# Two token streams on one core: another order for convolution, attention and MLP of the second stream

## The chip, the cores and the metric

The kernel runs on one core of one Trainium2 chip. A core has five engines that work beside each other and meet at semaphores: TensorE (PE: matmuls), VectorE (DVE), ScalarE (ACT), GpSimd (POOL) and SyncE (SP, which here issues DMA transfers). Each engine takes its own instructions strictly in the order in which the program put them into its queue. The metric is the device time of one execution in microseconds. Three timed runs of the kernel before gave a median of 3942.52 us (3938.76 to 3944.16).

## What is computed

One inference step of a two-layer decoder for a prompt of 1024 tokens and eight samples of eight tokens. Cut to its core:

```
for layer in (0, 1):
    x += conformer_conv(rms_norm(x))  if layer == 0 else  rwkv7_time_mix(rms_norm(x))
    x += cross_attend(rms_norm(x), memory K/V of the layer)     # 4 heads, 256 memory tokens
    x += sq_relu_mlp(rms_norm(x))                               # 1024 -> 4096 -> 1024
y = rms_norm(x)
```

The convolution module is a product 1024 -> 2048 with a gate, a causal depthwise convolution of 31 taps, a LayerNorm, and a product 1024 -> 1024. The RWKV module is a set of products (r, k, v and low-rank ones), a recurrence over positions with a 64x64 state per head (the scan), and an output product. All values are fp32; weights that are read for several products are split into a high and a low part, and each product is three matmuls (high by high, high by low, low by high).

## The kernel before, in words

The 1088 tokens are cut in two parts. Part 1 (512 tokens) is stream A, part 2 (576 tokens: 512 of the prompt and the 64 of the samples) is stream B. Activations lie with channels on the partitions; a matmul takes a 128x128 piece of a weight and 256 (A) or 288 (B) tokens. A product over 1024 channels is 24 such matmuls into one PSUM bank (`prod`, lines 126 to 128), then an evacuation on ACT or DVE. A weight tile of 128x1024 comes by a 512 KB DMA, ACT rounds it (line 95) and DVE or POOL takes the remainder (line 96).

Each stream runs through the same stages, one after the other. Names as used below, with the lines that show in the profile:

- convolution (`convolve`: fp32 matmuls L345 and L425 on PE, the other taps as 25 or 23 DVE passes per channel group, L441 and L444), then its output (`conv_out`: a LayerNorm, L470 to L490, and a product whose bank is added to x by DVE, L496);
- first attention (`attention`: for each of 8 units scores, softmax, four transposes L541, output; then a product added to x by DVE L288; stream B has the samples' caches besides, L590 to L593, and needs 32 more weight tiles for them);
- first MLP (`mlp`: 3,072 matmuls per stream; up banks through ACT L692, POOL L694 and the pair `u`, down banks added to x by DVE L708);
- the inputs of the RWKV module (`projections`: norm, token mixing on POOL, DVE and ACT, three products of 384 matmuls each, and low-rank products L792 and L841);
- the scan (lines 1070 to 1500: banks `p_pp`, `p_pz`, `p_py`; units of 2 head pairs and 256 tokens, 8 for A, 8 and one for the samples for B; the second matmul of a unit's last step, L1441, is used below as the mark of its end);
- memory keys of layer 1 (A alone), output product, second attention, second MLP and the last norm.

The streams are two generators. `pace` calls the one whose clock is behind; what a generator yields is the cost that is added to its clock, and `scaled` multiplies it:

```
i = min(ready, key=lambda i: clock[i])
c = next(gens[i], "end")
clock[i] += c
```

Stream B's factors stand in `CONV_COST` (convolution and its output) and `B_COST` (first attention, first MLP, RWKV inputs, output, second attention). A larger factor means that B is called less often beside the same piece of A. B's scan waits for the end of A's scan. The order of these calls is the order of priority; a scheduler then places the instructions of each engine, and may put a later one first where an earlier one isn't ready by its own reckoning. The scan is emitted 1000 places ahead in priority. So the tables set an order, not a time, and what stands in the queues has to be read from the built program.

Of the kernel before, what the change touches and what calls it, by code (L numbers as in the profile page):

```python
# [155 lines left out]
def body(tc, nc, es, a, o):  # L156
# [37 lines left out]
    def use_part(ctx, s, name):  # L194

        n = PARTS[s.part][1]
        s.use_ring([(s.pool(ctx, "ring" + name), "w", RING.get(s.name + name, 2))])
        hp = s.pool(ctx, "part" + name)
        s.x1 = hp.tile([P, NC8, 1 + n], F32, name="x" + s.name + name)
        s.x = xt[s.part] = s.x1[:, :, 1:]  # L200
        s.hp = hp
# [5 lines left out]
    def load_x(part, src, tiles=None):  # L207
        for t0, n in tiles or PARTS[part][2]:
            nc.sync.dma_start(out=xt[part][:, :, t0:t0 + n], in_=src[:, :, t0:t0 + n])
# [721 lines left out]
    def prior(gen, key):  # L931
        by = AHEAD.get(key, 0)
        return ahead(gen, by) if by else gen

    def scaled(gen, by):
        for c in gen:
            yield c if isinstance(c, str) else by * (1.0 if c is None else c)
# [12 lines left out]
    def conv_layer(s):  # L950
        with ExitStack() as ph:
            s.phase(ph, "c", d=4)
            cq = s.pool(ph, "cq")
            yield from convolve(s, cq, s.part)
            yield f"conv{s.part}!"
            yield from conv_out(s, s.part, pair(s))

    def att_layer(s, l, **k):
        with ExitStack() as ph:
            s.phase(ph, f"a{l}", **(dict(d=2, sa=2) if s.part else dict(d=4)))  # L960
            ap = s.pool(ph, f"at{l}")
            yield from attention(s, ap, l, s.part, pair(s), 1, (ap, "kv", 1))

    def mlp_layer(s, l):
        with ExitStack() as ph:
            s.phase(ph, f"m{l}", d=4 if s.part or l == 0 else 4)
            u = s.pool(ph, f"u{l}").tile([P, 2, 4, PARTS[s.part][1]], F32R, name="u")
            if l and s.part:
                s.use_ring(s.ring + [(s.pool(ph, "rx"), "w", 2)])
            yield from mlp(s, l, s.part, pair(s), u)  # L970
            if l:
                yield from final(s, s.part)

    def rwkv_in(s):
        with ExitStack() as ph:
            yield from projections(s, ph, s.part, pair(s))
# [6 lines left out]
    def rwkv_out(s):  # L983
        with ExitStack() as ph:
            s.phase(ph, "wo", d=4)
            yield from mixer_out(s, s.pool(ph, "yl"), s.part, pair(s))
# [27 lines left out]
    def second():  # L1014
        s = sB
        with ExitStack() as ph:
# [8 lines left out]
            load_x(1, a["x"][:, :, 512:])  # L1025
            yield from scaled(prior(conv_layer(s), "convB"), CONV_COST)
            yield OFFSET
            yield from scaled(prior(att_layer(s, 0), "att0B"), B_COST[0])
            yield "att0B!"
            yield from scaled(prior(mlp_layer(s, 0), "mlp0B"), B_COST[1])  # L1030
            yield "mlp0B!"
            yield from scaled(prior(rwkv_in(s), "inB"), B_COST[2])
            yield "in0B!"
# [3 lines left out]
        with ExitStack() as ph:  # L1037
            use_part(ph, s, "1")
            yield from scaled(prior(rwkv_out(s), "outB"), B_COST[3])
            yield from scaled(prior(att_layer(s, 1), "att1B"), B_COST[4])  # L1040
            yield "att1B!"
# [6 lines left out]
TAP_COST = 0.353  # L1048
OFFSET = 5.0
SCAN_COST = [1.344, 1.248]  # L1050
B_COST = [1.1, 1.0, 1.075, 1.04, 0.85]
MLP_COST = 1.0
EVERY = {'Bc': 4, 'Aa0': 3}
RAWS = 4
# [6 lines left out]
MEM_COST = 3.0  # L1061
MEM1 = True
SCAN_AHEAD = 1000
CONV_COST = 0.96
TMP = dict(A=dict(acc=2, sq=2, rs=2, h=2, sg=2, ev=2, dl=2, st=2), B=dict(h=2, sg=2, ev=2, sq=2), Bp=dict(dl=2, st=2), Bm0=dict(sg=2))
PE_PAIRS = (4, 3)
BUF = dict(w=5, ld=1, Z2=2, bon=2, ar=2, Aq=2, UV=2, AV=2, BK=1, pcs=2)
# [604 lines left out]
```

## Time and profile before

| | |
|---|---|
| median of three runs | 3942.52 us |
| the profiled execution | 3943.05 us, its span 3941.3 us |
| PE busy | 3729.5 us (95%), 29898 matmuls |
| DVE, ACT, POOL busy | 62%, 41%, 21% |
| mean granted TensorE clock | 0.949 of full |

A time axis in the text is microseconds from the start of the span. Matmul records overlap, so a busy PE is not one at its peak: the number of matmuls in a stretch (x) and the granted clock (1.00 is 2.4 GHz, 0.50 is 1.2 GHz, in between a mix of both) say more than the busy share. Stages of stream A by the first and last of their matmuls: convolution and its output 14 to 372, first attention to 674, first MLP to 1303, RWKV inputs to 1743, scan to 2337. B's scan ends at 3026.

### The profile page before, as it was taken

The numbers are of one execution on the slowest core, as the hardware profiler recorded it, in microseconds if no ns is written. First come the engines' busy times: TensorE is split into PE (matmuls) and PEld (weight loads), VectorE is DVE, ScalarE is ACT, GpSimd is POOL, SyncE is SP. The second block draws the span as 40 slices with busy tenths as digits, with TensorE's granted clock in tenths as the row PEclk, the third lists the DMA queues.
The fourth block names the chain that finished last, engine by engine and source line by source line (L and its number), as shares of the span: only waits on it lengthen the run. The fifth ranks groups of instructions, "written<-read, shape, count | busy, mean of one in ns | idle before, by whom it ended". The sixth has DMA issues, their size and how long they took to land. (4 is left out here: it accounts for less than half of the span.)

```text
span 3941.3 us, 74158 instructions
## 1 busy us (share of the span) xinstructions
PE 3729.5 (95%) x29898; PEld 3440.5 (87%) x29898; DVE 2456.6 (62%) x4800; ACT 1628.7 (41%) x3347; POOL 844.6 (21%) x1084
## 2 busy tenths in 40 slices
PE   8989979999999999998999978898999999999998
PEld 7757769999999999998788756787889999999998
DVE  7889964556554765457787736867774445753334
ACT  3233253445333444444465543454544335532222
POOL 0010121024101333211464311222121003301110
PEclk9999989999999999999699968898999999999998
DMA  6424223245322333332133326322223335532221
GB/s 220 129 57 136 72 83 110 83 136 186 118 79 93 117 118 120 123 124 93 55 111 100 103 83 225 111 68 76 69 79 121 116 104 164 169 99 81 84 83 52
DMA packets 231864, 428.64 MB, mean 109 GB/s; under 512 B 42848, under 2 KB 151648, under 8 KB 231520
## 3 DMA queue, kind: packets, MB, share of 16 engines
q1 hardware_dynamic: 202592, 392.95, 31.2%
q10 hardware_dynamic: 27648, 26.75, 2.0%
q8 instruction: 235, 3.85, 0.4%
q0 software_dynamic: 1280, 4.20, 0.3%
q14 instruction: 109, 0.89, 0.1%
HBM read 354.43 MB, written 60.91 MB: 105 GB/s over the span
## 5 line engine op out<-in xcount | busy, mean ns | idle before, releaser
L96 DVE TENSOR_TENSOR wt<-raw,wt 128x1024 fp32r<-128x1024 f32 x471 | 599.2, 1275 | 414.0 <-ACT wt L95 411.9
L95 ACT CAST wt<-raw 128x1024 fp32r<-128x1024 f32 x512 | 533.6, 1047 | 493.1 <-PE B_d L128 249.0
L126 PE MATMUL B_d<-hAB,wt 128*128 128x288 f32 (+1 forms) x2240 | 674.6, 304 | 18.4 <-ACT hAB L95 7.1
L127 PE MATMUL B_d<-hBB,wt 128*128 128x288 f32 (+1 forms) x2240 | 673.0, 301 | 6.6 <-DVE hBB L96 6.4
L128 PE MATMUL B_d<-hAB,wt 128*128 128x288 f32 (+1 forms) x2240 | 668.4, 299 | 2.3 <-DVE wt L96 2.3
L126 PE MATMUL A_d<-hAA,wt 128*128 128x256 f32 x2240 | 640.6, 289 | 24.2 <-ACT hAA L95 21.4
L128 PE MATMUL A_d<-hAA,wt 128*128 128x256 f32 x2240 | 633.2, 285 | 14.1 <-DVE wt L96 11.9
L127 PE MATMUL A_d<-hBA,wt 128*128 128x256 f32 x2240 | 639.5, 287 | 6.4 <-DVE hBA L96 6.4
L126 PEld LDWEIGHTS A_d<-hAA,wt 128*128 128x128 f32 x2240 | 427.9, 192 | 40.1 <-ACT hAA L95 26.7
L126 PEld LDWEIGHTS B_d<-hAB,wt 128*128 128x128 f32 x2240 | 427.7, 192 | 29.3 <-ACT hAB L95 10.9
L128 PEld LDWEIGHTS A_d<-hAA,wt 128*128 128x128 f32 x2240 | 427.4, 192 | 20.9 <-DVE wt L96 13.0
L127 PEld LDWEIGHTS A_d<-hBA,wt 128*128 128x128 f32 x2240 | 428.3, 192 | 19.6 <-DVE hBA L96 9.0
L127 PEld LDWEIGHTS B_d<-hBB,wt 128*128 128x128 f32 x2240 | 429.8, 192 | 11.7 <-DVE hBB L96 9.1
L694 POOL TENSOR_TENSOR t_sg<-t_ev 128x256 f32<-128x256 f32 (+1 forms) x256 | 184.8, 722 | 1160.3 <-ACT t_ev L692 1096.5
L128 PEld LDWEIGHTS B_d<-hAB,wt 128*128 128x128 f32 x2240 | 429.3, 192 | 4.0 <-DVE wt L96 2.9
L126 PE MATMUL B_d<-u,wt 128*128 128x288 f32 x1024 | 302.1, 296 | 0.7 <-DVE xB L708 0.7
L127 PE MATMUL B_d<-u,wt 128*128 128x288 f32 x1024 | 301.5, 296 | 0.0
L128 PE MATMUL B_d<-u,wt 128*128 128x288 f32 x1024 | 300.9, 296 | 0.4 <-DVE wt L96 0.4
L128 PE MATMUL A_d<-u,wt 128*128 128x256 f32 x1024 | 287.8, 283 | 0.7 <-DVE wt L96 0.7
L127 PE MATMUL A_d<-u,wt 128*128 128x256 f32 x1024 | 288.1, 282 | 0.0
L126 PE MATMUL A_d<-u,wt 128*128 128x256 f32 x1024 | 287.3, 283 | 0.0
L96 DVE TENSOR_TENSOR u<-t_sg,u 128x256 fp32r<-128x256 f32 (+1 forms) x256 | 131.6, 516 | 140.7 <-ACT u L95 140.4
(401 smaller groups left out, 7545.8 us busy)
## 6 DMA issues: line engine op xcount, KB each, us to landing
raw<-in_mlp_up_dram SPq DMA_DIRECT2D x128, 512.0 KB, 3.4
raw<-in_mlp_dn_dram SPq DMA_DIRECT2D x128, 512.0 KB, 3.4
raw<-in_rw_w_dram SPq DMA_DIRECT2D x64, 512.0 KB, 3.5
ld<-scr SPq DMA_DIRECT2D x32, 640.0 KB, 5.5
wf<-in_w_in_dram SPq DMA_DIRECT2D x32, 512.0 KB, 3.5
raw<-in_xa_w_q_dram SPq DMA_DIRECT2D x32, 512.0 KB, 3.4
raw<-in_xa_w_o_dram SPq DMA_DIRECT2D x32, 512.0 KB, 3.5
raw<-in_ck_dram SPq DMA_DIRECT2D x32, 512.0 KB, 3.5
```

The lines of the kernel that those rows point to most:

```text
L95: self.nc.scalar.copy(hi, src)
L96: (engine or self.nc.vector).tensor_tensor(lo, src, hi.bitcast(F32), SUB)
L126: self.nc.tensor.matmul(out, lhsT=wh, rhs=mh, start=(i == 0), stop=False)
L127: self.nc.tensor.matmul(out, lhsT=wh, rhs=ml, start=False, stop=False)
L128: self.nc.tensor.matmul(out, lhsT=wl, rhs=mh, start=False, stop=(i == last))
L694: nc.gpsimd.tensor_mul(sg[:, :n], r[:, :n], r[:, :n])
```

## The change

Three numbers of the tables, and nothing else:

```
-B_COST = [1.1, 1.0, 1.075, 1.04, 0.85]
+B_COST = [0.9, 0.5, 1.075, 1.04, 0.85]
-CONV_COST = 0.96
+CONV_COST = 2.0
```

B's convolution and its output are called at about half the rate, its first attention at 1.22 times and its first MLP at twice the rate; the factors of the later stages stay. No instruction is added or removed: each engine has the same instructions in another order. Three places in the built programs follow. In all of them A_ and xA are stream A's banks and residual, B_ and xB stream B's.

The first place is DVE's queue where B's convolution output is added to x (L496). Before, it stands among A's attention (L525 to L534 are a softmax, `pr` and `hBA<-A_d` the unit's splits):

```order
L487 TENSOR_TENSOR xB_145<-xB_145,t_rs 128x288 x8
L525 TENSOR_REDUCE st_3896<-A_d 128x2
L496 SCALAR_TENSOR_TENSOR xB_145<-B_d,vec,xB_145 128x288
L96 TENSOR_TENSOR hBB<-t_h,hAB 128x288 x2
L529 RECIPROCAL st_3896<-st_3896 128x2
L534 TENSOR_SCALAR e<-e,st_3896 128x256 x2
L496 SCALAR_TENSOR_TENSOR xB_145<-B_d,vec,xB_145 128x288
```

In the changed program the first of them stands among the down products of A's first MLP (L708):

```order
L708 TENSOR_TENSOR xA_103<-xA_103,A_d 128x256 x4
L96 TENSOR_TENSOR wt<-raw,wt 128x1024
L496 SCALAR_TENSOR_TENSOR xB_145<-B_d,vec,xB_145 128x288
L96 TENSOR_TENSOR u<-t_sg,u 128x256
L96 TENSOR_TENSOR wt<-raw,wt 128x1024
L96 TENSOR_TENSOR u<-t_sg,u 128x256 x2
L496 SCALAR_TENSOR_TENSOR xB_145<-B_d,vec,xB_145 128x288
```

All 384 matmuls of B's convolution output moved behind the first matmul of A's first MLP; before, 264 of them stood in front of the last one of A's first attention. The convolution itself did not move: PE's queues agree but for a few neighbours up to place 1823, which the trace of before reaches at 544 us, and that is behind the last of B's convolution.

The second place is PE's queue at the end of the third unit of A's scan (`p_` rows are the scan's). Before, B's RWKV inputs stand between its rows (`hAB`, `hBB`, and the low-rank `B_hd`):

```order
L126 MATMUL B_d<-hAB,wt 128x288
L1441 MATMUL p_py<-rs,c_bones 128x512
L1329 MATMUL p_pp<-td,Ybd 128x16 x8
L792 MATMUL B_hd<-hc,w_21397 128x288
L792 MATMUL B_hd<-hc,w_21397 64x288
L127 MATMUL B_d<-hBB,wt 128x288
```

Now B's first MLP stands there (`u`):

```order
L126 MATMUL B_d<-u,wt 128x288
L1441 MATMUL p_py<-rs,c_bones 128x512
L127 MATMUL B_d<-u,wt 128x288
L128 MATMUL B_d<-u,wt 128x288
L126 MATMUL B_d<-u,wt 128x288
L127 MATMUL B_d<-u,wt 128x288
L1329 MATMUL p_pp<-td,Ybd 128x16 x8
```

Of the 3,084 matmuls of B's first MLP and its norm 551 stand behind the first matmul of A's scan before, and 1,837 now.

The third place is PE's queue at the end of A's scan. Before, memory keys of stream A follow at once:

```order
L1389 MATMUL p_py<-Aq,UV 64x64 x2
L1436 MATMUL p_py<-y,c_bones 128x512
L1441 MATMUL p_py<-rs,c_bones 128x512
L126 MATMUL A_d<-hAA,wt 128x256 x2
L127 MATMUL A_d<-hBA,wt 128x256
```

Now the rest of B's RWKV inputs follows:

```order
L841 MATMUL B_d<-lh,w_23724 128x288
L1441 MATMUL p_py<-rs,c_bones 128x512
L792 MATMUL B_hd<-hc,w_23585 64x288
L792 MATMUL B_hd<-hc,w_23694 128x288
L792 MATMUL B_hd<-hc,w_23694 64x288
L126 MATMUL B_d<-hAB,wt 128x288
```

397 of the 1,436 matmuls of B's RWKV inputs stand behind the end of A's scan now, none before.

Split matmuls (those that read a weight tile `wt`) in front of the end of each scan unit, counted from the one before it, in both programs; the first count starts at the first matmul of A's scan:

| end of unit | before | after |
|---|---|---|
| A 1 | 551 MLP B | 605 MLP B |
| A 2, 3, 4 | 60, 334, 230 inputs B | 329, 358, 321 MLP B |
| A 5 | 198 inputs B | 224 MLP B |
| A 6, 7, 8 | 186, 144, 0 inputs B | 401, 223, 240 inputs B |
| samples | 288 memory A, 83 output A | 288 inputs B, 288 memory A, 384 output A |
| B 1 | 301 output A, 114 attention A | 411 attention A |
| B 2, 3, 4, 5 | 282, 96, 135, 333 attention A | 81, 164, 304 attention A, 324 MLP A |
| B 6, 7, 8 | 285, 330, 382 MLP A | 371, 354, 343 MLP A |

## Rows read from the trace of the kernel before

**Rows 1.** Page, parts 1 and 2: busy time, PE and granted clock in 40 slices
```profile
PE 3729.5 (95%) x29898; PEld 3440.5 (87%) x29898; DVE 2456.6 (62%) x4800; ACT 1628.7 (41%) x3347; POOL 844.6 (21%) x1084
...
PE   8989979999999999998999978898999999999998
...
PEclk9999989999999999999699968898999999999998
```

**Rows 2.** Busy time by stage: stretch, length, each engine's us, clock, DMA
```profile
14.00:372.00 358.00, 334.61 (x1706) 265.56 (x1707) 311.82 (x528) 116.29 (x262) 24.79 (x45) 0.97 0.40 125
372.00:674.00 302.00, 270.45 (x1682) 231.89 (x1680) 219.02 (x391) 113.96 (x235) 56.48 (x46) 0.93 0.29 93
674.00:1303.00 629.00, 623.38 (x5060) 618.81 (x5058) 341.38 (x609) 258.11 (x471) 118.42 (x138) 0.99 0.36 116
1303.00:1743.00 440.00, 439.55 (x3380) 429.95 (x3379) 256.12 (x463) 192.70 (x461) 129.93 (x209) 1.00 0.40 124
1743.00:2337.00 594.00, 546.89 (x5020) 471.03 (x5021) 413.70 (x957) 299.33 (x692) 228.40 (x347) 0.86 0.28 90
2337.00:3026.00 689.00, 627.33 (x6173) 543.28 (x6174) 457.24 (x1030) 312.86 (x631) 144.62 (x124) 0.91 0.32 102
3026.00:3942.00 916.00, 886.86 (x6889) 879.54 (x6887) 453.90 (x816) 330.05 (x586) 141.38 (x170) 0.98 0.34 110
```

**Rows 3.** The same view, instructions that touch a weight tile wt alone
```profile
613.00:628.00 15.00, 15.00 (x131) 15.00 (x131) 2.44 (x2) 4.20 (x4) 4.76 (x2) 1.00 0.37 117
3600.00:3900.00 300.00, 300.00 (x2263) 300.00 (x2262) 57.62 (x47) 48.24 (x47) 0.00 (x0) 1.00 0.24 76
```

**Rows 4.** As rows 3: the end of A's first attention
```profile
544.00:673.00 129.00, 111.95 (x822) 107.83 (x823) 14.69 (x12) 16.79 (x16) 8.07 (x4) 0.92 0.30 97
```

**Rows 5.** TensorE's waits in 372:700: us in total, times, longest
```profile
PE A_d L541 <- DVE e L534: 14.5, 6, 5.6
```

**Rows 6.** As rows 3, by scan unit, stream B's MLP or A's beside it
```profile
1743.00:1859.00 116.00, 82.56 (x551) 75.87 (x551) 15.76 (x13) 12.53 (x12) 0.00 (x0) 0.99 0.28 92
...
2587.00:2649.00 62.00, 39.82 (x285) 34.75 (x283) 10.03 (x8) 7.30 (x7) 0.00 (x0) 1.00 0.31 99
2649.00:2706.00 57.00, 16.45 (x96) 13.98 (x96) 2.71 (x2) 2.10 (x2) 0.00 (x0) 0.79 0.17 52
...
2763.00:2829.00 66.00, 44.86 (x333) 40.52 (x333) 8.53 (x7) 6.98 (x7) 0.00 (x0) 1.00 0.25 81
2829.00:2900.00 71.00, 39.91 (x288) 35.34 (x286) 7.30 (x6) 6.24 (x6) 0.00 (x0) 0.93 0.23 78
2900.00:2965.00 65.00, 44.85 (x330) 40.36 (x330) 8.56 (x7) 7.32 (x7) 0.00 (x0) 1.00 0.21 67
2965.00:3026.00 61.00, 50.92 (x383) 46.34 (x382) 9.80 (x8) 8.37 (x8) 0.00 (x0) 1.00 0.23 72
```

**Rows 7.** As rows 6, stream B's RWKV inputs beside the unit
```profile
1859.00:1925.00 66.00, 15.09 (x60) 11.82 (x60) 0.00 (x0) 0.00 (x0) 0.00 (x0) 0.63 0.17 55
1925.00:2014.00 89.00, 58.11 (x335) 50.85 (x334) 8.54 (x7) 7.35 (x7) 0.00 (x0) 0.84 0.30 92
2014.00:2098.00 84.00, 40.59 (x232) 35.46 (x230) 6.75 (x6) 6.29 (x6) 0.00 (x0) 0.92 0.34 106
2098.00:2162.00 64.00, 32.84 (x198) 28.46 (x198) 4.33 (x4) 3.15 (x3) 0.00 (x0) 0.97 0.34 108
2162.00:2236.00 74.00, 31.70 (x186) 27.45 (x186) 4.89 (x4) 4.20 (x4) 0.00 (x0) 0.91 0.30 95
```

**Rows 8.** As rows 6: the last unit of A, then up to the samples' unit
```profile
2295.00:2337.00 42.00, 0.00 (x0) 0.00 (x0) 0.00 (x0) 0.00 (x0) 0.00 (x0) 0.50 0.18 59
2337.00:2479.00 142.00, 69.62 (x371) 56.80 (x371) 23.52 (x18) 18.77 (x18) 0.00 (x0) 0.83 0.59 189
2479.00:2587.00 108.00, 61.11 (x415) 55.73 (x415) 12.95 (x10) 10.46 (x10) 0.00 (x0) 0.87 0.30 94
```

**Rows 9.** One POOL line of the scan, in 1760:1850
```profile
L1186 POOL TENSOR_TENSOR bk<-ld 128x512 f32<-128x512 f32 x2 | 3.3, 1632 | 10.3 <-DVE ld L1185 10.3
```

**Rows 10.** The same line in 1925:2098
```profile
L1186 POOL TENSOR_TENSOR bk<-ld 128x512 f32<-128x512 f32 x2 | 5.5, 2766 | 1.6 <-DVE ld L1185 1.6
```

## The prediction

> **What bounds the kernel now.** I read the page first: PE is busy 95% of the span, all others far less, and the chip shows two kinds of slices: most at full clock, and two regions with less, around slices 5 to 7 and 18 to 29 [rows 1]. So TensorE is the engine to look at, and the question is where it is not at its peak. The busy times by stage answer it [rows 2]. The reader is to compare matmuls per microsecond and the clock: A's first MLP (674 to 1303) and A's RWKV inputs (1303 to 1743) run at clock 0.99 and 1.00 with PE busy throughout; the two scan stages (1743 to 3026) run at 0.86 and 0.91, the end of A's first attention at 0.92 [rows 4]. A dense stretch gives the price of work: 2,263 matmuls of stream B in 300 us are 0.1326 us each, 131 of stream A in 15 us are 0.115 us [rows 3]. By these prices a stage's split matmuls can be set against its length; what is left over is what the stage loses. For the scan this goes by unit. Beside an MLP or an attention a unit takes its companion's matmuls plus 27 to 38 us: 66 less 333 x 0.115 is 28, 65 less 330 x 0.115 is 27, 62 less 285 x 0.115 is 29, 71 less 288 x 0.115 is 38 (there the MLP's norm begins) [rows 6]; with few companions it still takes 57. Beside B's RWKV inputs it is 38 to 53: 89 less 335 x 0.1326 is 45, then 53, 38 and 49; and at their beginning 66 less 60 x 0.1326 is 58, at clock 0.63 [rows 7].
>
> **The change part by part.** Nothing is added, so each term is work that lies elsewhere. Counts of matmuls in the changed program are from the built order.
>
> 1. *B's convolution at half pace.* PE's queue is the same up to the place reached at 544 us, behind the convolution. Cost: nothing, and no wait changes.
>
> 2. *B's convolution output leaves A's first attention.* From 544 to 673 there were 822 split matmuls, 516 of them A's. A's own are 516 x 0.115 = 59 us, B's 306 x 0.1326 = 41 us, so 129 - 100 = 29 us were lost, mostly between the attention's units, where PE waits for the softmax (14.5 us in 6 waits) [rows 4, 5]. Now A stands alone. In the first half of this stretch B's matmuls filled gaps that stay, and then A's output product needs no filler: of the 41 us I take 29 as saved here. They come back as 41 us among A's first MLP, a dense stage. Term: +12 us. Bounds: 0 (all 41 saved) and +25 (16 saved).
>
> 3. *B's first MLP leaves the front.* 1,837 - 551 = 1,286 of its matmuls go behind the beginning of A's scan. They ran in dense stages, at 0.1326 us: -171 us. What they covered stays covered: A's first MLP has B's output product and attention beside it, A's inputs have attention and then MLP at twice the pace.
>
> 4. *B's first attention beside A's RWKV inputs.* 836 of its 1,276 matmuls lie there now, before they were all beside A's first MLP. Both use POOL and DVE in short chains. DVE was busy 256 of 440 us there and POOL 130 [rows 2], so neither queue is full. Trace and program show no stage of this kind, so bounds: 0 us, as the attention cost beside the MLP, and +47 us, if the stretch, some 210 us of matmuls by the order, loses at the rate of rows 4 (29 in 129). Taken: +12, nearer to the dense rows. With that A's scan begins at 1743 + 12 - 171 + 12 = 1596.
>
> 5. *A's scan beside B's MLP.* Unit 1: 116 us with 551 matmuls, now 605: 123. Units 2 to 4: 329, 358, 321 matmuls and 30.5 us each (mean of the four above): 74 + 78 + 73 = 225. Unit 5 has 224 of the MLP (30 + 30), and the beginning of B's inputs, for which I add 20 (the 58 of rows 7 less 38): 80. Units 6 and 7 with 401 and 223 matmuls of B's inputs at 46 us each (mean of four): 99 and 76. Unit 8: 240 matmuls are 32, and the scan's remainder, which took 42 us alone [rows 8], partly beside them: 67. Sum 670, before 594: +76.
>
> 6. *From there to the samples' unit.* Before: 142 us with 371 matmuls [rows 8]. Added are the tail of B's inputs (288 matmuls, 38 us, and its low-rank products, about 13 more) and 301 of A's output product (35 us), half of which I let fill gaps. B's scan can't begin before these inputs are stored and read back, as before. 142 + 51 + 22 = 215: +73. Bounds: +45, +100.
>
> 7. *B's eight units.* Before 547 us. Now 108, 57, 57, 65, 75, 73, 71, 56 by the same prices = 562: +15. In exchange 1,400 - 1,005 = 395 matmuls of A's last MLP are done by the end of B's scan and leave the dense tail [rows 2]: -45.
>
> 8. *Queues and transfers.* 1,286 matmuls are 27 weight tiles (48 matmuls each); with them 27 DMAs on SP, 27 casts on ACT and 27 remainders on DVE move into A's scan stage. By rows 3 a remainder is 57.62/47 = 1.23 us: 33 us on DVE, plus some 22 us of evacuations, on top of 414 in 594 [rows 2]: about 70% of 670 us. The DMA share there is 0.28. No cost.
>
> Sum: 3941.3 - 147 + 76 + 73 + 15 - 45 = 3913; the execution was 1.75 us longer than its span and 0.5 us above the median, which makes no difference: **3915 us**. Its own range, by the bounds above and the spread of the unit prices (27 to 38 over three units, 38 to 53 over three), is 3880 to 3950.
>
> **The rivals.**
>
> *B's RWKV inputs keep their own pace (slower).* Before, they were spread over A's units 2 to 8, from 1859 to 2295: 436 us. The forecast gives them some 320 us, in units 5 to 8 and the tail behind. If their chain (POOL, DVE, ACT, DVE per channel group) and not PE set those 436 us, up to 116 us come on top, and all else stands behind them in PE's queue: 4030 in full, 3970 at half. It makes the change slower once they need over about 355 us. For it: beside them one POOL pass of the scan takes 2,766 ns against 1,632 ns beside the MLP [rows 9, 10], so engines hold each other up. Against: DVE is not full, and their matmul rate rose to 3.8 per us in unit 3 (335 in 89 us). The Trainium skill (GPSIMD Engine Reference, section Key points) says that POOL shares its SBUF interfaces with DVE and is slowed by DVE operations with two SBUF inputs. By that rule, denser mixing would stretch itself, and the time would go towards the 4030; rows 9 and 10 agree in direction, with two instances each.
>
> *The scan stage gives all of it back (no change).* The front alone at its upper bounds, 25 and 47 in place of 12 and 12, makes 3963; half of that excess, 3939. For it: before and after, the same scan chain and the same inputs have to run, and the saving of 171 us at the front is dense time, which nothing else made better. Against: units 2 to 4 have companions at 27 to 30 us, where they had 45 to 58.
>
> *The scan stage has more room than I give it (much faster).* If B's inputs cost a unit no more than an MLP does, units 5 to 7 lose 20 + 16 + 16 us less and the step behind some 15: 3848. For it: units beside an MLP run at clock 0.93 to 1.00 [rows 6], and PE's records of weight loads fill 471 of the 594 us, its matmuls 547 [rows 2]. Against: four units in rows 7, none under 38. The Trainium skill (Perfetto Trace Analysis, section Identifying the Most-Contended Engine) holds matmul occupancy a poor measure of what is left on TensorE, and weight-load occupancy a better one. By the first 47 us are free in A's scan stage, by the second 123; the second would hide most of the 171 us that come and give about the time of this rival, while the unit prices, which are measured waits, say less.
>
> **How the numbers follow.** A measurement of this kernel can tell about 0.2%, 8 us, from no change: faster is under 3934.6, slower over 3950.4. The forecast's band under 3935 has 0.45, the fast rival 0.13, no change 0.19, slower 0.23. That gives 0.58, 0.19 and 0.23. The range from 3855 to 3980 leaves out the far ends of the first and the third rival, about 0.1 each.
>
> **What would show it.** Right: A's scan begins near 1596 with A's first MLP and inputs at clock 0.99 or more; units 2 to 4 at 72 to 80 us; the end of B's scan near 3045, the tail some 45 us shorter. Step 2 is wrong if A's first MLP begins before 650 or after 685; step 4 if A's inputs take over 470 us; step 5 if a unit beside the MLP takes over 85 us. The slow rival shows as more than 355 us from the first to the last matmul of B's inputs; the fast one as units 5 to 7 under 80 us. A scan stage (both scans) longer than 1,500 us, against 1447 here, would make the forecast wrong whatever the front does.

## The result and the profile after

The changed kernel is slower: 4077.71 us (median of 4 runs, 4077.21 to 4085.95) against 3940.64 us (4 runs), ratio 1.0352 with the 95% interval 1.0327 to 1.0376. 3915 us had been forecast. The profiled execution has a span of 4084.0 us, 171 more than the 3913 of the forecast's sum.

The page after, same lines as [rows 1]:

```profile
PE 3820.0 (94%) x29898; PEld 3491.2 (85%) x29898; DVE 2467.9 (60%) x4800; ACT 1630.8 (40%) x3347; POOL 853.5 (21%) x1084
...
PEclk9989969999998999999878997888999899999998
```

DVE and POOL are busy 11 and 9 us longer than before, by no more than 1.1%, with the same instructions. PE is busy 90 us longer with the same 29,898 matmuls and idle 52 us longer, and 12 slices have a clock under nine tenths, where 7 had. So no work was added: there are stretches where PE got its matmuls more slowly. Busy time by stage, columns as in [rows 2]; the bounds are the same events (A's convolution with its output, first attention, first MLP, RWKV inputs, scan, B's scan, the tail):

```profile
13.00:374.00 361.00, 336.47 (x1714) 267.20 (x1715) 314.91 (x534) 117.18 (x266) 25.53 (x47) 0.97 0.41 127
374.00:648.00 274.00, 231.24 (x1363) 194.67 (x1361) 196.17 (x357) 99.94 (x214) 53.72 (x42) 0.88 0.26 81
648.00:1131.00 483.00, 475.28 (x3899) 472.96 (x3898) 227.22 (x426) 165.57 (x304) 51.03 (x70) 0.99 0.30 97
1131.00:1667.00 536.00, 492.00 (x3568) 466.39 (x3566) 330.78 (x575) 254.73 (x564) 189.10 (x248) 0.95 0.43 134
1667.00:2362.00 695.00, 668.39 (x5906) 581.14 (x5906) 453.97 (x1005) 306.99 (x674) 223.33 (x328) 0.93 0.25 81
2362.00:3192.00 830.00, 767.89 (x6972) 669.84 (x6971) 507.63 (x1118) 361.84 (x752) 173.63 (x182) 0.90 0.33 103
3192.00:4084.00 892.00, 848.75 (x6490) 838.99 (x6490) 434.41 (x784) 319.70 (x565) 136.57 (x162) 0.97 0.33 108
```

The reader is to see the fourth row: A's RWKV inputs, dense before at clock 1.00, have 3,568 matmuls in 536 us, 6.7 per us, against 7.7 before. A's scan begins at 1667 where 1596 was forecast (+71); it lasts 695 for 670 (+25). The same scan by unit, matmuls that touch a weight tile, as [rows 6 to 8] (A's eight units, the step to the samples' unit, B's first unit):

```profile
1667.00:1787.00 120.00, 88.61 (x605) 81.55 (x605) 15.20 (x13) 13.57 (x13) 0.00 (x0) 1.00 0.24 78
1787.00:1856.00 69.00, 49.17 (x329) 44.53 (x329) 8.78 (x7) 7.13 (x7) 0.00 (x0) 1.00 0.25 81
1856.00:1934.00 78.00, 55.49 (x358) 48.57 (x357) 10.32 (x8) 7.48 (x8) 0.00 (x0) 1.00 0.24 79
1934.00:2010.00 76.00, 54.89 (x326) 45.63 (x324) 9.16 (x7) 7.28 (x7) 0.00 (x0) 0.97 0.23 74
2010.00:2102.00 92.00, 47.88 (x225) 36.94 (x225) 6.09 (x5) 5.23 (x5) 0.00 (x0) 0.80 0.23 77
2102.00:2216.00 114.00, 69.22 (x401) 58.07 (x401) 9.77 (x8) 8.38 (x8) 0.00 (x0) 0.87 0.25 81
2216.00:2303.00 87.00, 42.67 (x223) 34.95 (x223) 4.86 (x4) 4.82 (x5) 0.00 (x0) 0.82 0.25 78
2303.00:2362.00 59.00, 37.19 (x240) 32.76 (x240) 6.10 (x5) 4.63 (x5) 0.00 (x0) 1.00 0.33 106
2362.00:2619.00 257.00, 153.08 (x960) 136.59 (x960) 38.78 (x31) 32.27 (x31) 0.00 (x0) 0.85 0.56 174
2619.00:2737.00 118.00, 64.72 (x411) 57.22 (x411) 10.94 (x9) 9.39 (x9) 0.00 (x0) 0.89 0.21 68
```

Units 2 to 4, beside the MLP, took 69, 78 and 76 us for 74, 78 and 73 forecast. The misses lie behind them: units 5 to 8 together 352 for 322, the step to the samples' unit 257 for 215 (+42). B's eight units end at 3192, 573 us for 562 (+11), and the tail is 892 for 871 (+21). 71 + 25 + 42 + 11 + 21 make 170 of the 171. Both scans with the step between them took 695 + 257 + 573 = 1525 us: more than the 1,500 that the prediction named as the length at which it would be wrong whatever the front does.

One more reading brings the kernels of this study together. B's scan can begin when both A's scan and B's RWKV inputs are done. The later of these two ends is called the gate here; the span less the gate is nearly a constant:

| kernel | median us, ratio to before | A's scan, first matmul to end | B's inputs, first to last matmul | span less gate |
|---|---|---|---|---|
| before | 3940.64 | 1743-2339 | 1854-2320 (466) | 1602 |
| the change | 4077.71, 1.0352 | 1667-2362 | 2078-2471 (393) | 1613 |
| scan_only | 3956.85, 1.0038 [1.0023, 1.0053] | 1584-2219 | 1966-2343 (377) | 1610 |
| pair_only | 4060.52, 1.0298 [1.0281, 1.0315] | 1843-2431 | 1950-2411 (461) | 1628 |
| conv_only | 4022.47, 1.0205 [1.0190, 1.0221] | 1519-2122 | 2122-2564 (442) | 1457 |
| att_mlp_only | 4107.23, 1.0417 [1.0402, 1.0433] | 1995-2491 | 1686-2148 (462) | 1610 |
| cache_dve | 4059.37, 1.0310 [1.0292, 1.0327] | 1652-2356 | 2062-2454 (392) | 1603 |
| mix_dve | 4077.91, 1.0348 [1.0331, 1.0364] | 1664-2349 | 2070-2455 (385) | 1609 |
| dl4 | 4074.24, 1.0336 [1.0316, 1.0357] | 1663-2359 | 2080-2465 (385) | 1609 |
| cache_half | 4046.71, 1.0267 [1.0246, 1.0288] | 1638-2326 | 2047-2432 (385) | 1613 |
| cache_quarter | 4046.01, 1.0277 [1.0251, 1.0302] | 1626-2316 | 2037-2423 (386) | 1621 |
| no_samples | 4035.06, 1.0251 [1.0230, 1.0271] | 1620-2314 | 2021-2421 (400) | 1613 |
| in_fast | 4107.56, 1.0417 [1.0396, 1.0439] | 1668-2456 | 2066-2478 (412) | 1621 |
| mid1 | 3954.55, 1.0044 [1.0029, 1.0059] | 1668-2293 | 1910-2336 (426) | 1611 |
| mid2 | 3980.28, 1.0106 [1.0091, 1.0121] | 1670-2325 | 1902-2353 (451) | 1620 |
| before_mixb | 3990.81, 1.0118 [1.0093, 1.0142] | 1742-2355 | 1853-2331 (478) | 1637 |
| before_pool3 | 3985.82, 1.0131 [1.0100, 1.0162] | 1743-2349 | 1853-2326 (473) | 1626 |

(Stages are bounded by matmuls in the trace of one profiled execution of each kernel, an end at the end of the last one; a ratio is to runs of the kernel before on the same chip.) In 16 of 17 kernels 1,602 to 1,637 us follow the gate. conv_only is the exception: there A's second attention begins at 2317, 247 us in front of the gate (before at 2539, 200 us behind it), so less is left to do. The 35 us between 1,602 and 1,637 are also the limit of this reading: mid1 has its gate 3 us earlier than the kernel before and is 0.4% slower. The change moved the gate from 2339 to 2471, 132 of the 143 us by which its span grew.

### The profile page after: what moved, and what is told of

The parts are those of the page before. It is cut to its first block, busy times and chain, and to the rows that moved or that the text cites. A ratio compares the mean times of both kernels' runs of the same rounds, so it can differ in the third digit from the quotient of the medians.

```text
span 4084.0 us, 74154 instructions
## 1 busy us (share of the span) xinstructions
PE 3820.0 (94%) x29898; PEld 3491.2 (85%) x29898; DVE 2467.9 (60%) x4800; ACT 1630.8 (40%) x3347; POOL 853.5 (21%) x1084
## 5 line engine op out<-in xcount | busy, mean ns | idle before, releaser
L126 PE MATMUL B_d<-u,wt 128*128 128x288 f32 x1024 | 305.4, 300 | 2.8 <-DVE xB L708 2.8
L127 PE MATMUL B_d<-u,wt 128*128 128x288 f32 x1024 | 305.8, 301 | 0.0
L128 PE MATMUL B_d<-u,wt 128*128 128x288 f32 x1024 | 304.9, 300 | 0.0
```

Of the source, the lines that this page charges most:

```text
L126: self.nc.tensor.matmul(out, lhsT=wh, rhs=mh, start=(i == 0), stop=False)
L127: self.nc.tensor.matmul(out, lhsT=wh, rhs=ml, start=False, stop=False)
L128: self.nc.tensor.matmul(out, lhsT=wl, rhs=mh, start=False, stop=(i == last))
```

## The experiments

Where a kernel gives the first MLP two paces, `scaled` has two more arguments: the factor `by` holds until `upto` of the generator's own cost is spent, then `then`.

### Which half of the change costs: scan_only and pair_only

The first leaves convolution and attention as before and has only the MLP's move into A's scan:

```
-CONV_COST = 2.0                  +CONV_COST = 0.96
-B_COST = [0.9, 0.5, 1.075, ...]  +B_COST = [1.1, 1.0, 1.075, ...]
-yield from scaled(prior(mlp_layer(s, 0), "mlp0B"), B_COST[1])
+yield from scaled(prior(mlp_layer(s, 0), "mlp0B"), 2.47, 117, 0.5)
```

> Only the scan part of the change: B's convolution, its output and first attention are paced as before (attention beside A's first MLP), the first MLP at 2.47 times its cost up to A's scan and half of it from there, so that 1,818 of its matmuls lie behind the start of A's scan as in the changed kernel (1,837), and the later order is nearly the same. Theory 1 (in the changed kernel A's RWKV inputs are slow because B's attention runs beside them): they are dense here, A's first MLP begins near 674, A's scan near 1743 - 168 = 1575, and with the changed kernel's time from there (4084 - 1667 = 2417) the whole takes about 3992. Rival (A's RWKV inputs have a floor of their own and lacked other matmuls to hide it): the stage keeps 440 us or more with 1,079 matmuls of B beside it, A's scan begins at 1650 or later and the whole takes 4050 to 4080. Second rival (the front was free, all of the loss lies in the scan): 4080 too, but with A's scan begun at 1575.

The second has the changed convolution and attention, and the MLP in front of A's scan as before:

```
-yield from scaled(prior(mlp_layer(s, 0), "mlp0B"), B_COST[1])
+yield from scaled(prior(mlp_layer(s, 0), "mlp0B"), 0.23, 311, 1.3)
```

> Only the front of the change: convolution factor 2.0 and attention factor 0.9 as in the changed kernel, so B's attention lies beside A's RWKV inputs (836 matmuls), but the first MLP is called at 0.23 of its cost up to A's scan, so that only 553 of its matmuls are left for the scan, as before (551), and the scan stage has the order of before. Theory 1 (attention beside A's RWKV inputs costs by itself, by DVE and POOL): A's scan begins near 1743 + 70 = 1813 and the whole takes 4000 to 4015. Rival (A's inputs have a floor that other matmuls hide): with 2,531 matmuls of the MLP beside them the loss is covered, A's scan begins near 1755, 3955. Second rival (all of the loss lies in the scan): 3941 to 3950.

scan_only took 3956.85 us, +0.38%; pair_only 4060.52 us, +2.98%. The two excesses, 14 and 118 us, add up to 132, near the 137 of the whole change, so most of the loss comes with the new place of convolution output and attention. They add up in the total only: the gate moved by 4 and 92 us in these two and by 132 in the change, and 26 of pair_only's 118 us lie behind its gate. Stages of scan_only (A's inputs; A's scan; to the samples' unit):

```profile
1250.00:1571.00 321.00, 315.27 (x2421) 304.46 (x2420) 200.42 (x381) 152.09 (x391) 116.73 (x186) 0.99 0.42 129
1584.00:2219.00 635.00, 617.83 (x5849) 550.14 (x5847) 453.33 (x994) 302.73 (x664) 222.27 (x317) 0.96 0.27 87
2219.00:2493.00 274.00, 241.09 (x1610) 201.31 (x1610) 143.19 (x261) 106.77 (x224) 59.06 (x84) 0.85 0.52 165
```

With the MLP beside them A's inputs are dense (7.5 matmuls per us) and take 321 us, so they have no floor near 440: A's scan begins at 1584, 9 us later than the dense price says. Theory 1 is right in the front, and too pessimistic behind it (3992 expected). Of pair_only (B's attention with samples beside A's inputs; its output product; the switch to the MLP's norm; the MLP):

```profile
1133.00:1310.00 177.00, 138.26 (x981) 127.04 (x979) 146.83 (x228) 104.54 (x213) 110.44 (x124) 0.90 0.56 178
1310.00:1411.00 101.00, 100.85 (x772) 97.72 (x773) 53.18 (x94) 45.07 (x114) 30.25 (x53) 1.00 0.38 115
1411.00:1490.00 79.00, 68.16 (x444) 61.88 (x443) 53.72 (x124) 37.86 (x95) 22.94 (x33) 0.89 0.24 74
1490.00:1828.00 338.00, 338.00 (x2546) 333.70 (x2544) 134.39 (x221) 109.33 (x216) 41.06 (x64) 1.00 0.32 100
```

The reader is to see 981 matmuls in 177 us and 444 in 79 (5.5 and 5.6 per us), between dense stretches with 7.5 to 7.6. The last stretch, 2,546 matmuls of which some 2,160 are the MLP's, comes too late to help: the MLP follows attention in the same stream. A's scan begins 100 us late. Step 2 has 17 of that (312 matmuls of the convolution output at 0.1326 us come back, 41 us, and A's first MLP begins at 650 in place of 674); the other 83 are what it costs to have B's attention beside A's RWKV inputs, called the pairing from here on. The changed kernel agrees: A's first MLP begins 26 us earlier, so step 2 costs 15, its front saved 76 us, and 171 - 15 - 76 leaves 80. Both figures are what is left over when the other terms are taken at their prices.

### The two tables apart: conv_only and att_mlp_only

```
conv_only:      CONV_COST = 2.0    B_COST = [1.1, 1.0, 1.075, 1.04, 0.85]
att_mlp_only:   CONV_COST = 0.96   B_COST = [0.9, 0.5, 1.075, 1.04, 0.85]
```

> Only the convolution factor 2.0; the other factors as before. B's attention lies beside A's inputs as in the changed kernel (880 matmuls), but 2,893 of the first MLP's matmuls lie behind the start of A's scan (317 to 350 beside each unit) and B's RWKV inputs wholly behind A's scan, beside A's output and second attention; A's last MLP lies beside B's scan. By the unit prices: A's scan begins near 1667 - 140 = 1527, eight units 116 + 7 x 72 = 620, to the samples' unit 153 + 226 + 60 = 440, eight units of B 576, tail 892 - 195 + 60 = 757, together 3920. If A's RWKV inputs have a floor of their own they end later, 1600 to 1650, and the whole takes 3990 to 4040. Either way the first scan should show that beside the MLP alone a unit loses 27 to 38 us.

> Only the factors of B's attention and first MLP (0.9 and 0.5); the convolution factor as before. B's stream runs ahead: its whole first MLP and 975 matmuls of its RWKV inputs lie in front of A's scan, which has only 461 matmuls beside it. By the unit prices: A's scan begins at 1743 + (551 + 975) x 0.1326 = 1945, its units cost 57 us each with nothing beside them, about 100 + 7 x 57 = 500, then 142, 547 and 916 as before: 4050. Theory 1 in its wide form (two mixing or attention chains beside each other slow each other on DVE and POOL) adds some 50 us where B's RWKV inputs lie beside A's: 4100.

conv_only in the pairing stretch, in A's scan, and from there to the samples' unit:

```profile
1130.00:1330.00 200.00, 163.98 (x1143) 150.73 (x1143) 161.09 (x248) 119.11 (x256) 125.74 (x150) 0.90 0.53 169
1519.00:2122.00 603.00, 594.58 (x5919) 541.83 (x5919) 383.97 (x852) 251.66 (x493) 127.58 (x131) 0.99 0.23 75
2122.00:2690.00 568.00, 530.56 (x3960) 485.59 (x3958) 368.15 (x701) 277.43 (x629) 184.13 (x306) 0.94 0.47 147
```

The same pairing shows the same rate (5.7 per us). Beside the MLP alone A's scan runs at clock 0.99 and 603 us, 17 less than by the unit prices: those prices hold. What failed is the step behind: 568 us where 440 were expected, because B's inputs, called behind A's scan, took 442 us. att_mlp_only came out at 4107, as the wide form of theory 1 has it (4100): A's scan begins at 1995, 50 us behind the dense price, where B's inputs lie beside A's. So each of the two tables costs by itself: the convolution's 2.05% (1.90 to 2.21), the other 4.2%.

### What holds the pairing up: cache_dve, mix_dve, dl4

The changed kernel from 1131 to 1310 us, columns as for the stages:

```profile
1131.00:1310.00 179.00, 142.91 (x995) 131.72 (x994) 149.32 (x230) 106.33 (x214) 111.04 (x124) 0.89 0.55 176
```

DVE is busy 149 of 179 us, PE has 995 matmuls. The main groups there on POOL and then DVE (group, busy us, mean ns, idle before and what ended it):

```profile
L754 POOL TENSOR_TENSOR t_dl<-xA 128x256 f32<-128x256 f32 x51 | 41.5, 822 | 26.0 <-DVE hBA L96 21.9 <-DVE hc L96 4.1
L96 POOL TENSOR_TENSOR wt<-raw,wt 128x1024 fp32r<-128x1024 f32 x15 | 40.4, 2695 | 8.0 <-ACT wt L95 8.0
...
L759 DVE SCALAR_TENSOR_TENSOR t_dl<-t_dl,vec,xA 128x256 f32<-128x256 f32 x51 | 42.0, 834 | 7.7 <-POOL t_dl L754 7.7
L96 DVE TENSOR_TENSOR wt<-raw,wt 128x1024 fp32r<-128x1024 f32 x30 | 39.4, 1319 | 9.2 <-ACT wt L95 9.1
```

45 remainders of weight tiles pass in 179 us, 15 of them on POOL at 2.7 us, between the steps of A's token mixing. In scan_only's A inputs, where POOL takes no remainder, the mixing step on DVE is a third shorter:

```profile
L96 DVE TENSOR_TENSOR wt<-raw,wt 128x1024 fp32r<-128x1024 f32 x43 | 53.4, 1246 | 37.9 <-ACT wt L95 37.8
L759 DVE SCALAR_TENSOR_TENSOR t_dl<-t_dl,vec,xA 128x256 f32<-128x256 f32 x96 | 52.2, 559 | 19.7 <-POOL t_dl L754 19.2
```

PE itself waits in many short pieces, the longest sums for stream B's operands, then for A's (the changed kernel, same stretch; total us, times, longest):

```profile
PE B_d L541 <- DVE e L534: 5.4, 4, 2.5
PE B_sa L593 <- DVE wt L96: 4.9, 2, 4.1
PE B_d L127 <- DVE pr L96: 4.1, 2, 2.2
...
PE A_d L126 <- ACT hAA L95: 2.9, 3, 1.4
```

Three kernels changed what the queues hold:

```
cache_dve  -... nc.gpsimd if hp else None) for n in ("ck", "cv")
           +... nc.gpsimd if hp and l else None) for n in ("ck", "cv")
mix_dve    -nc.gpsimd.tensor_sub(dl[:, :n1], ...)
           +(nc.gpsimd if part else nc.vector).tensor_sub(dl[:, :n1], ...)
dl4        -TMP = dict(A=dict(..., dl=2, st=2), ...)
           +TMP = dict(A=dict(..., dl=4, st=2), ...)
```

> The changed kernel with one thing else: in B's first attention the remainders of the samples' caches that POOL took (16, of which 15 lie in the slow stretch from 1131 to 1310 us at 2,695 ns each, 40 us of POOL) are taken by DVE (1,319 ns each there, about 20 us more on DVE). Theory P (POOL holds up A's token mixing: its subtractions queue behind these long passes): the stretch becomes shorter, A's scan begins near 1635 in place of 1667, the whole takes 4035 to 4055. Theory V (DVE, busy 149 of 179 us there, is the engine that both chains wait for): the stretch becomes longer, 4085 to 4105. If neither engine but the hand-overs between them set it: within 10 us of 4078.

> The changed kernel with one thing else: the subtraction of the token mixing of A's RWKV inputs (51 in the slow stretch, 822 ns each on POOL, 41 us) is done on DVE, so that a mixing step is DVE, ACT, DVE without the hand-over from POOL; about 51 x 0.35 = 18 us more on DVE there. Theory P (POOL and the hand-over are late): A's scan begins 20 to 40 us earlier, 4040 to 4058. Theory V (DVE is the bound): 10 to 20 us later, 4088 to 4100.

> The changed kernel with four buffers in place of two for the tile t_dl of stream A's token mixing (dl=4). In the slow stretch POOL's subtractions wait 21.9 us in 16 waits for DVE to release t_dl, and the copies and remainders of B's attention are queued behind them on POOL. Theory Q (queues in order: one stream's waiting step holds up the other's): the stretch loses 20 to 40 us less, A's scan begins at 1627 to 1647 (1667 in the changed kernel), the whole takes 4040 to 4058. Theory V (the amount of DVE work sets the stretch): no change, 4070 to 4085.

The stretch from 1131 to 1310 in cache_dve, and two groups of DVE in it:

```profile
1131.00:1310.00 179.00, 153.53 (x1116) 142.73 (x1114) 149.16 (x258) 112.30 (x235) 87.40 (x124) 0.91 0.58 188
```

```profile
L96 DVE TENSOR_TENSOR wt<-raw,wt 128x1024 fp32r<-128x1024 f32 x47 | 58.4, 1255 | 11.9 <-ACT wt L95 11.7
L759 DVE SCALAR_TENSOR_TENSOR t_dl<-t_dl,vec,xA 128x256 f32<-128x256 f32 x56 | 30.7, 562 | 6.6 <-POOL t_dl L754 6.4
```

in mix_dve:

```profile
1131.00:1310.00 179.00, 143.14 (x1033) 133.07 (x1033) 164.45 (x290) 108.14 (x225) 79.85 (x77) 0.91 0.55 181
```

and in dl4:

```profile
1131.00:1310.00 179.00, 143.34 (x1066) 133.46 (x1064) 162.42 (x246) 110.63 (x232) 128.41 (x139) 0.92 0.56 186
```

cache_dve gained 18 us (A's scan at 1652), the other two nothing in the total (1664 and 1663). DVE took 17 more remainders and was not busy longer, because its other instructions became shorter; the mixing step fell from 834 to 562 ns. Single instructions of the changed kernel show how. The first line is POOL's, the others DVE's (start and length in us):

```profile
1210.92 2.42 POOL L96 TENSOR_TENSOR wt<-raw,wt 128x1024 fp32r<-128x1024 f32 x1 [0.91 <-ACT wt L95]
...
1209.07 0.47 DVE L759 SCALAR_TENSOR_TENSOR t_dl<-t_dl,vec,xA 128x256 f32<-128x256 f32 x1
...
1211.02 2.62 DVE L759 SCALAR_TENSOR_TENSOR t_dl<-t_dl,vec,xA 128x256 f32<-128x256 f32 x1
```

The first mixing step takes 0.47 us. The second begins 0.1 us into POOL's pass and ends 0.3 us after it. In 13 of POOL's 15 remainder passes here one DVE instruction, of a mixing step or of another kind, lasts in this way until the pass is over, 2.1 to 2.8 us; together the 13 take some 26 us more than the same instructions with POOL idle. The 17 remainders that DVE took over cost it some 21. mix_dve and dl4 kept POOL's 15 passes, and 12 and 13 DVE instructions are still held; in mix_dve most of them are others than the mixing step, whose mean is 575 ns there. The Trainium skill (GPSIMD Engine Reference, section Key points) names DVE and POOL as sharing their SBUF interfaces; the 834 and 562 ns agree.

So theory P is right for 15 us and no more. With the hand-over gone (mix_dve) DVE fills to 164 of 179 us, a subtraction taking 512 ns where 350 had been reckoned, and neither theory's time came (4077.91); a deeper buffer does not help either, as theory V has it.

### Weights, or any attention: cache_half, cache_quarter, no_samples

These leave work out: cache_half uses one of a sample's two cache tiles for both halves, cache_quarter one tile for two samples and both halves, no_samples drops the samples' attention and copies their queries through (the pacing cost is kept).

```
cache_half  -kt, = caches.take(1)
            +kt, = caches.take(1) if hp == 0 or l else (kt,)
no_samples  +if samples is not None and l == 0:
            +    s.split(oA[:, :, samples:], oB[:, :, samples:], q[...])
            +    todo = [lambda: iter([1.3, 1.3])] * 18
```

> The changed kernel without half of the samples' caches: in B's first attention the tile of each sample's first half is used for the second half too, so 16 of the 32 tiles (16 DMAs, 16 casts on ACT and the 16 remainders on POOL) are left out; the matmuls are all there. In the slow stretch this takes 40 us of 111 from POOL, about 16 from ACT and nothing from DVE. Theory W (the weights of the samples' attention, which serve few matmuls each, overload POOL and DVE beside the mixing): the stretch loses 30 to 50 us less, 4030 to 4050. Theory V (DVE alone): as with the remainders on DVE, which gained 18, about 4060. Theory C (the chains of hand-overs of the two streams, with no matmuls that are ready ahead): 4055 to 4075.

> The changed kernel with 8 of the 32 cache tiles of the samples' attention: one tile serves two samples and both halves, so 24 DMAs, 24 casts on ACT and 24 remainders (16 on POOL, 8 on DVE) are left out; the matmuls are all there. With half of the tiles left out A's scan began 29 us earlier (1638 for 1667). Theory W (the cost of the pairing is the weight work of the samples' attention, by its amount): 40 to 50 us earlier, 1617 to 1627, the whole 4025 to 4037. If the first half took all that this work costs: 1635 to 1640 again, 4044 to 4050.

> The changed kernel without the samples' part of B's first attention: the samples' columns are copied from their queries, and scores, softmax and output of the samples with their 32 cache tiles are left out (some 268 matmuls, about 30 us of PE work at the dense price); the cost that paces the streams is kept, so 568 matmuls of B's attention still lie beside A's RWKV inputs. Theory W: apart from the 30 us of work the loss in the stretch from 1131 to 1330 us (about 65 us against dense prices in the changed kernel) falls to 10 or 20, as where B's RWKV inputs lie beside A's second attention; A's scan begins at 1585 to 1600. Theory C (any attention beside the inputs loses that much by its chain of softmax and transposes): only the 30 us go, A's scan begins at 1630 to 1640.

The same stretch in cache_half:

```profile
1131.00:1310.00 179.00, 160.46 (x1230) 151.87 (x1229) 135.29 (x256) 103.61 (x236) 83.04 (x130) 0.96 0.47 152
```

in cache_quarter:

```profile
1131.00:1310.00 179.00, 170.55 (x1337) 163.27 (x1336) 132.95 (x260) 102.10 (x245) 77.15 (x134) 0.98 0.42 136
```

and in no_samples:

```profile
1131.00:1310.00 179.00, 156.93 (x1135) 147.30 (x1134) 124.46 (x249) 94.79 (x233) 65.51 (x106) 0.93 0.38 124
```

995 matmuls in the changed kernel become 1,230 and 1,337 as 16 and 24 tiles go; A's scan begins 29 and 41 us earlier. So about half of the pairing's 80 us is the weight work of the samples' attention: each tile costs a DMA, a cast and a remainder and feeds only 8 matmuls, where a tile of a product feeds 48. The tiles took all three with them, so only the remainders on POOL are tested by themselves (cache_dve, 15 us); what the DMAs and the casts cost is not told apart. In the total the second step, from 16 to 24 tiles left out, is worth nothing: cache_quarter took 4046.01 us, cache_half 4046.71, because the time behind the gate is 8 us longer there.

Without any samples' matmuls the rate falls again, and A's scan begins only 6 us before that of cache_quarter, though its last 8 tiles and 256 matmuls, some 30 us, are gone: these matmuls had been filling gaps. A's scan at 1620 lies between the two theories (1585 to 1600, 1630 to 1640). With few tiles the stretch is nearly dense, 7.5 matmuls per us in cache_quarter, so a good part of what is left of the pairing must lie elsewhere. One such place is the switch from B's attention to the norm of its MLP, in the changed kernel and in cache_quarter:

```profile
1404.00:1485.00 81.00, 73.09 (x490) 66.13 (x489) 62.01 (x133) 42.04 (x102) 26.60 (x36) 0.92 0.30 93
1371.00:1451.00 80.00, 72.90 (x470) 66.94 (x468) 55.89 (x122) 37.15 (x92) 22.38 (x31) 0.87 0.26 85
```

Here 490 and 470 matmuls take 80 us, 6 per us, with the tiles or without most of them. Why, and whether this makes up the rest, was not tested.

### The length of B's inputs: in_fast, mid1, mid2

```
in_fast  B_COST = [0.9, 0.5, 0.6, 1.04, 0.85]    (the rest as the change)
mid1     CONV_COST, B_COST as before; first MLP 1.55, 170, 0.45
mid2     as mid1; first MLP 1.4, 193, 0.5; B_COST[2] = 0.95
```

> The changed kernel with the factor of B's RWKV inputs at 0.6 in place of 1.075: the built order puts all their 1,436 matmuls in front of the end of A's scan (444, 360, 202 and 146 beside the last four units) and gives the units 3 and 4 more of the MLP. In seven kernels so far everything behind the last matmul of B's inputs took 1,610 to 1,648 us. Floor theory (the inputs need some 377 to 393 us however dense they are called): they begin near 2040, end at 2420 to 2440, the whole takes 4035 to 4060. Rate theory (PE's order sets their length): they end near 2340, the whole takes 3950 to 3990.

> Convolution and attention as before, B's first MLP paced at 1.55 up to A's scan and 0.45 from there, so that 1,132 of its matmuls lie behind the start of A's scan (551 before, 1,818 in the kernel with only the scan part, 1,837 in the change): it lasts up to the third unit, and B's RWKV inputs follow at 216 to 264 matmuls a unit and end with A's scan. Theory (without the pairing the scan takes MLP matmuls well, and what the kernel with only the scan part lost was the wait for B's inputs behind A's scan, its samples' step being 273 us against 141): A's scan begins at 1743 - 581 x 0.1326 = 1666, lasts about 630, samples' step 153, B's units 555, tail 908: 3913. Rival (the scan stage gives back what the front saves whatever the split): 3940 to 3957.

> As the kernel before in this set, with the MLP at 1.4 and then 0.5 (1,087 matmuls behind the start of A's scan) and B's RWKV inputs at 0.95 in place of 1.075, so that they end a unit earlier, with units 5 and 6 at 312 and 240 matmuls and the last two units at 240 and 144. Theory: A's scan begins near 1672, the samples' step is as short as before (141 to 150), 3910 to 3920. Rival as there: 3940 to 3957.

in_fast is worse than the change (1.0417): called densely, B's inputs took 412 us, more than the 393 of the change. Its third and fourth unit, with 445 and 458 matmuls of the MLP beside them:

```profile
1858.00:1958.00 100.00, 100.00 (x764) 88.22 (x763) 51.14 (x115) 33.41 (x62) 16.29 (x18) 0.93 0.20 69
1958.00:2084.00 126.00, 123.12 (x857) 99.89 (x855) 53.90 (x134) 41.70 (x85) 14.12 (x19) 0.88 0.24 80
```

Here 100 - 445 x 0.1326 is 41 and 126 - 458 x 0.1326 is 65, where units 2 to 4 of the change, with 326 to 358, lose 25 to 33. PE is idle for 3 us in these two units together, and why a unit loses more with more companions is open. The rate theory (3950 to 3990) is refuted: PE's order alone doesn't set the length of B's inputs. The floor theory was nearer, but the inputs ended at 2478 where it had 2420 to 2440, and the total came out some 50 us above it. mid1 and mid2 looked for a gain with a smaller move and no pairing. A's scan began at 1668 and 1670, as expected, and lasted 625 in mid1 (630 expected), yet they took 3954.55 and 3980.28 us: B's inputs ended at 2336 and 2353, near the 2343 of scan_only. The rival (3940 to 3957) was right for mid1; mid2, whose inputs were called more densely as well, is 23 us above it. In all three the front's saving is lost at the gate, which stays within 14 us of where it was.

### Which engine the inputs beside the scan want: before_mixb, before_pool3

```
before_mixb   -nc.gpsimd.tensor_sub(dl[:, :n1], ...)
              +(nc.vector if part else nc.gpsimd).tensor_sub(dl[:, :n1], ...)
before_pool3  EVERY = {'Bc': 4, 'Aa0': 3, 'Bp': 3}
```

> The kernel before with the subtraction of the token mixing of B's RWKV inputs on DVE in place of POOL. Beside these inputs a unit of A's scan cost 38 to 53 us above its companions' matmuls, 27 to 38 beside an MLP, and POOL passes of the scan took 2,766 against 1,632 ns. If POOL and its hand-over make that difference, units 2 to 7 lose some 10 us each less: B's inputs end near 2260 and the whole takes 3880 to 3900. If not, 3935 to 3955.

> The kernel before with every third remainder of the weights of B's RWKV inputs on POOL in place of DVE (about 9 of 27). With the mixing's subtraction moved from POOL to DVE the kernel before became 50 us slower, with DVE busy 55 to 76 us of a unit of 67 to 97, so DVE work beside the scan has a price. If that holds the other way: 10 to 25 us faster, 3915 to 3930. Rival (a POOL pass of 2.7 us holds up the scan's own POOL passes and slows DVE's): 3945 to 3970.

Both were slower, by 1.2% and 1.3%, more than either side of the two expectations had: the kernel with work moved from POOL to DVE lost, and the one with work moved from DVE to POOL as well. The order of other instructions moved with both edits (B's inputs in unit 7 fell from 144 split matmuls to 72 and 120), so this does not name the engine; that stays open. No kernel beat the one before.

## Why the prediction was wrong

Steps 1 to 3 held in the main. The convolution did not move (its matmuls L345 and L425 lie from 224 to 476 us in both). A's first attention ended as bare as step 2 says, 503 matmuls in 104 us at clock 0.79 where [rows 4] has 822 in 129:

```profile
544.00:648.00 104.00, 71.50 (x503) 68.45 (x503) 8.57 (x7) 9.42 (x9) 4.79 (x2) 0.79 0.27 84
```

A's MLP began at 648. By step 2's own sum, 29 of 41 us saved, it had to begin at 674 - 29 = 645; the limits that the prediction named for it, 650 and 685, contradict that sum. Step 2 cost about +15 for +12. The price of step 3 is confirmed by scan_only: its front saved 159 us where that price gives 168.

**Step 4 failed**: B's attention beside A's RWKV inputs was taken at +12 us, with an upper bound of +47. It cost 80 to 83 us. The argument was that DVE and POOL had idle time in [rows 2], a mean over a stage in which B's MLP supplied the matmuls. In the changed kernel the counts are others: 45 weight tiles in 179 us for 995 matmuls, with DVE busy for 149 us, some 26 of them held by POOL's passes. About half of the 80 us went when 24 of the 32 cache tiles were left out; the other half is located in part and not explained. The rate of [rows 4], from which the bound came, had no samples' caches in it. The condition set for this step (A's inputs over 470 us) came true: 536.

**Steps 5 and 6** were the second miss, as the slow rival has it: B's inputs keep a length of their own. The forecast gave them some 320 us, and the rival's sign was more than 355. They took 393 here, and from 377 to 478 in all seventeen kernels, for each factor from 0.6 to 1.075 and in each place that was tried. The samples' unit ends 126 to 154 us behind the gate in all of them (2471 and 2621 here, 2339 and 2480 before). B's inputs begin 411 us after A's scan, where the forecast's terms give 378 or some more (123 + 225 and the last 224 matmuls of the MLP, 30), and last 73 us longer; that covers the 25 and the 42. What sets their length is not shown: the rival's chain of POOL, DVE and ACT was not confirmed by before_mixb and before_pool3. Step 6 also has a slip, 22 us for half of 35, which made the forecast some 5 us longer and is no part of the miss. Units 2 to 4, beside the MLP, were priced rightly; conv_only confirms it for eight units. scan_only shows that this miss alone turns the gain into +14 us: A's scan ended 120 us earlier there (2219 for 2339), and then 124 us passed until B's inputs were done (2343).

The fast rival fell: units 5 to 7 took 92, 114 and 87 us, none under 80. The Trainium skill (Perfetto Trace Analysis, section Identifying the Most-Contended Engine) would look for TensorE's room in weight-load occupancy, 581 of 695 us in A's scan now. How much of the rest can be used hangs on what lies beside the scan: 114 us stayed unused here, 61 of 603 in conv_only, where it is the MLP alone. Step 7's +15 for B's units was +26 (573 for 547), and its tail saved 24 us for 45. Nothing shows step 8's queues in the way of the MLP: DVE was busy 454 of 695 us in A's scan, and units 2 to 4 ran as forecast.

## What to carry to other kernels

Before two stages are laid beside each other, count for both what each needs per matmul from the side engines, and do not trust the idle time that these engines show beside another partner. Two pairs of stages that both prepare their operands on DVE or POOL did not fill each other's gaps here: B's attention beside A's RWKV inputs (80 us lost) and B's RWKV inputs beside A's (50 us, att_mlp_only). Find the event that the rest hangs on (here the later of two ends, with 1,602 to 1,637 us behind it in 16 kernels) and ask of each move only whether that event comes earlier. A saving in a stage ahead of it is worth nothing if another chain then holds the gate: B's inputs took 377 us or more wherever they were put.

## What the hardware showed unexpectedly

- A DVE instruction that began just before or within one of POOL's 2.7 us remainder passes lasted until the pass was over: 13 in 15 passes, the usual case ending 0.28 us after it, 2.6 us for an instruction that takes 0.47 us with POOL idle. When the passes went to DVE, DVE did 17 more remainders in the same 149 us.
- A unit of A's scan with 326 to 358 matmuls of the MLP lost 25 to 33 us, with 445 and 458 it lost 41 and 65, at clock 0.93 and 0.88 in place of 0.97 to 1.00 and with PE idle for 3 us in both together. The cause is open.
- Leaving out the samples' 256 matmuls, some 30 us, and their last 8 tiles in a stretch that waits let A's scan begin 6 us earlier (no_samples and cache_quarter).
